# Hybrid encoder layer on one core: first norm on ScalarE, token tiles in pairs, early reload of the gated activations

## The chip, the cores and the metric

One core of a Trainium2 chip runs the whole layer in one launch. The metric is the device time of that launch in microseconds; runs of one kernel are told by their median. Engines: TensorE (PE; its weight loads PEld), VectorE (DVE), ScalarE (ACT), GpSimd (POOL), and SyncE (SP), whose queue issues all the DMAs.

## The reference, cut to what matters

```python
h   = layer_norm(DEEPNORM_ALPHA * x + mixed @ w_out, ln1_g, ln1_b)
up  = depthwise_conv(h @ w_up, conv_w, conv_b)          # 3 taps over tokens
a, val = split(up, 2)
out = layer_norm(DEEPNORM_ALPHA * h + (gelu(a, exact) * val) @ w_down, ln2_g, ln2_b)
```

All float32; 1024 tokens, model width 1024, hidden width 2816. `mixed` is the gated sum of a state-space branch and an attention branch. Everything ahead of `mixed @ w_out` (the first 750 us) is the same in both kernels.

## The kernel before

A tile framework places the instructions: it schedules the program with a timeline model of its own, so the order on every engine is its choice and moves when the code changes. Each float32 product is made of three reduced-precision products (hi·hi, hi·lo, lo·hi), so every operand is split: ScalarE copies it to the high part (`whi`, `ghi`, `t1h`), and VectorE or GpSimd subtracts that from the raw value (`wlo`, `glo`, `t1l`; `split`, L161).

**Out-projection** (`out_projection`). Eight token tiles of 128 go in three groups, (0,1,2), (3,4,5), (6,7), each with its own pass over the eight weight blocks `wo`; a tile needs two accumulators `pso` of 128x512. After a group, each tile is normed: `r` is loaded from x (L1046; three buffers), VectorE adds the accumulators (L156, two operations), takes the moments, and applies the norm with its gain and bias in four more operations (L156); the result is stored to DRAM as `hd` (L1051). PE transposes it (`ptr`, eight 128x128 per tile, four to an accumulator, L1055), and ScalarE copies four at a time into H (`hraw`, transposed hidden state, L159). For tiles 0 to 3 `b0h` and `b0l`, the split of tokens 0 to 511, are made from the accumulator too.

**Up-projection** (`up_projection`). 22 column blocks j, each with seven products of 12 matmuls (L1111) in a Strassen-like scheme: `first` and `second` use b11 and b21 (tokens 0 to 511, in `b0h`/`b0l`) directly, the other five use `t1`, `t2`, `t3`, `t4`, which are differences of quadrants of H (rows 0-511 or 512-1023 of the width, tokens 0-511 or 512-1023), and `b22`. For j = 0 and 1 `first` and `second`, 48 matmuls, come before the sums; then the differences are made over all tokens at once on VectorE and split on ScalarE, VectorE and GpSimd. Weight blocks come through a ring of three buffers (`raw`, `whi`, `wlo`). After each j, ScalarE and VectorE do the convolution on the accumulators (`cv`), and the gated result goes to DRAM as Gd[j].

**Down-projection** (`down_projection`). The same three groups of tiles; for each of 22 blocks k Gd[k] is read back (`graw`, L1229), split into `ghi` and `glo`, and multiplied with `wd` (L1277 to L1279). After a group each tile's `r2` (two buffers, loaded from `hd`, L1253) gets ALPHA and the accumulators, then the second norm and the store to the output.

Of the kernel before, what the change touches and what calls it, by code (L numbers as in the profile page):

```python
# [8 lines left out]
F32 = mybir.dt.float32  # L9
F32R = mybir.dt.float32r  # L10
# [52 lines left out]
def constants():  # L63
# [10 lines left out]
    small = np.zeros((P, 24), np.float32)  # L74
# [10 lines left out]
def prepare(inp):  # L85
# [46 lines left out]
    o["cbig"], o["csm"] = constants()  # L132
    return o


class K:
# [70 lines left out]
    def run(self, upto="all"):  # L207
        tc, nc, A = self.tc, self.nc, self.A
        with ExitStack() as ctx:
# [15 lines left out]
            self.csm = csm = cst.tile([P, 24], F32, name="csm")  # L225
# [684 lines left out]
    def layer_norm(self, r, g, b, wk, done, cols=(slice(0, 512), slice(512, 1024))):  # L910
# [9 lines left out]
        nc.vector.reciprocal(sd, sd)  # L920
        for h in range(2):
# [86 lines left out]
    def ffn(self, right):  # L1008
        with ExitStack() as ch:
# [6 lines left out]
            H = chr_.enter_context(self.pool("hraw", 1)).tile([P, KT, S], F32, name="hraw")  # L1016
            self.out_projection(b0, H)
            right.close()
            tp = ch.enter_context(self.pool("tp", 1, side="right"))
            self.up_projection(b0, H, tp, chr_)  # L1020
            chh.close()
        self.down_projection()

    def out_projection(self, b0, H):
        nc, A, tt = self.nc, self.A, self.tt
        mh, ml = self.mh, self.ml
        with ExitStack() as cx:
            wk = cx.enter_context(self.pool("owk", 3))
            lw = cx.enter_context(self.pool("lw", 1))
            pt = cx.enter_context(self.pool("ptr", 2, space=PSUM))  # L1030
            po = [cx.enter_context(self.pool(f"po{z}", 1, space=PSUM)) for z in range(6)]
            bank = {0: 0, 1: 2, 2: 4, 3: 0, 4: 2, 5: 4, 6: 0, 7: 2}
            gb = lw.tile([P, 2, D], F32, name="lngb")
            for z in range(2):
                nc.sync.dma_start(gb[:, z], A["ln"][z:z + 1].partition_broadcast(P))
            for tiles in ((0, 1, 2), (3, 4, 5), (6, 7)):
# [7 lines left out]
                for i in tiles:  # L1044
# [5 lines left out]
                    def transposed(q, c):  # L1050
                        nc.sync.dma_start(self.hd[i][:, c], r[:, c])  # L1051
                        tr = pt.tile([P, 4, P], F32, tag="t", name="ptr")
                        for j in range(4):
                            k = 4 * q + j
                            nc.tensor.transpose(tr[:, j], r[:, P * k:P * k + P], self.ident)  # L1055
                        rows = (slice(None), slice(4 * q, 4 * q + 4), slice(P * i, P * i + P))
# [7 lines left out]
    def up_projection(self, b0, H, tp, chr_):  # L1064

# [230 lines left out]
```

## Time and profile before

| what | value |
|---|---|
| median of 3 runs (lowest, highest) | 1544.2 us (1543.13, 1544.93) |
| the profiled execution, its own time | 1542.73 us |
| its span in the profile | 1540.6 us |
| granted TensorE clock, mean | 0.982 |
| PE busy | 1462.9 us, 95% of the span |
| VectorE, ScalarE, GpSimd busy | 982.4, 635.5, 634.8 us |
| chain that ended last, largest shares | PE 66%, VectorE 7%, DMA 3% |

A row of the timeline gives the start, the length, the engine, the line of the kernel, the operation with its result and operands, a count, and in brackets how long the engine stood idle before it and what it was waiting for. `x4` after a row means four such operations one behind the other, with their length together. Lines are those of the kernel before; in the changed kernel the same helpers stand two lines lower (L148, L158, L161, L165), the product is L1132, the transposes L1067.

### The profile page before, as it was taken

How to read it: one execution, taken by the hardware profiler on the slowest of the kernel's cores; microseconds unless marked ns; L12 is line 12 of the kernel's file. 1: busy time of each engine (PE TensorE's matmuls, PEld its weight loads, DVE VectorE, ACT ScalarE, POOL GpSimd, SP SyncE). 2: the span in 40 equal slices, each digit the busy share in tenths (PEclk: the TensorE clock that was granted, in tenths of full speed). 3: DMA queues.
4: the chain of work that ended last, by engine and by line, in shares of the span. 5: the costliest groups of instructions: out<-in, count | busy, mean ns of one | idle time of the engine just before them, and what ended most of it. 6: DMA issues, size and time to landing. Idle time of an engine off the chain costs nothing.

```text
span 1540.6 us, 19832 instructions
## 1 busy us (share of the span) xinstructions
PE 1462.9 (95%) x7210; PEld 1207.6 (78%) x7210; DVE 982.4 (64%) x1654; ACT 635.5 (41%) x1029; POOL 634.8 (41%) x363
## 2 busy tenths in 40 slices
PE   8989999989999998999997699999999998999998
PEld 6878778888877776788876478888888886888876
DVE  8967888460036367532588888888888884362363
ACT  5346675202154434543344444444444444433030
POOL 1397784353113101655544333344444334924020
PEclk9999999999999999999999799999999999999999
DMA  7643453765326123433565022222222227666141
GB/s 262 167 111 95 121 138 119 232 195 157 103 73 199 60 63 106 132 119 96 191 193 195 32 72 87 87 86 86 82 82 83 82 83 254 220 195 189 46 153 36
DMA packets 98691, 195.81 MB, mean 127 GB/s; under 512 B 11809, under 2 KB 45601, under 8 KB 98465
## 3 DMA queue, kind: packets, MB, share of 16 engines
q1 hardware_dynamic: 98592, 194.55, 40.1%
q8 instruction: 56, 0.92, 0.3%
q14 instruction: 43, 0.34, 0.1%
HBM read 145.87 MB, written 48.63 MB: 126 GB/s over the span
## 4 chain that ended last, share of the span: by engine, by line
PE 66%; DVE 7%; DMA 3%; issue 1%; ACT 1%; SPq 1%; POOL 1%; POOLq 0%; DVEq 0%; ACTq 0%
PE psup L1111 26%; PE psg L178 11%; PE pso L1277 6%; PE pso L1278 6%; PE pso L1279 6%; PE psv L178 6%; DVE r L156 2%; PE pso L178 2%; PE psS L178 1%; PE psab L178 1%; DVE hraw L146 1%; PE psp L181 1%; DMA og<-atd 1%; DMA raw<-wup 1%; DMA raw<-wd 0%
## 5 line engine op out<-in xcount | busy, mean ns | idle before, releaser
L163 POOL TENSOR_TENSOR wlo<-raw,whi 128x1024 fp32r<-128x1024 f32 x143 | 358.4, 2512 | 588.5 <-ACT whi L159 452.5
L159 ACT ACTIVATE whi<-raw 128x1024 fp32r<-128x1024 f32 (+1 forms) x174 | 174.5, 1004 | 259.4 <-PE psg L178 64.3
L178 PE MATMUL psg<-xh,whi 128*128 128x512 f32 x448 | 180.6, 403 | 4.5 <-DVE vout L146 4.3
L178 PE MATMUL psg<-xl,whi 128*128 128x512 f32 x448 | 180.0, 402 | 0.0
L178 PE MATMUL psg<-xh,wlo 128*128 128x512 f32 x448 | 179.5, 401 | 0.0
L1278 PE MATMUL pso<-wlo,ghi 128*128 128x512 f32 (+1 forms) x374 | 142.3, 381 | 2.5 <-POOL wlo L163 2.5
L1277 PE MATMUL pso<-whi,ghi 128*128 128x512 f32 (+1 forms) x374 | 136.8, 384 | 6.0 <-ACT ghi L159 5.6
L1279 PE MATMUL pso<-whi,glo 128*128 128x512 f32 (+1 forms) x374 | 140.2, 379 | 0.0
L163 DVE TENSOR_TENSOR glo<-graw,ghi 128x384 fp32r<-128x384 f32 (+1 forms) x66 | 58.9, 898 | 123.9 <-ACT ghi L159 110.4
L156 DVE SCALAR_TENSOR_TENSOR cv<-psup,cwt,cv 128x1023 f32<-128x1023 f32 x88 | 112.8, 1282 | 38.7 <-ACT cv L159 37.2
L178 PEld LDWEIGHTS psg<-xh,whi 128*128 128x128 f32 x448 | 85.6, 191 | 26.8 <-DVE vout L146 5.0
L178 PEld LDWEIGHTS psg<-xh,wlo 128*128 128x128 f32 x448 | 85.7, 191 | 20.6 <-issue 3.1
L824 DVE CUSTOM_DVE_ANT_0 sm<-psS,cbig 128x256 f32<-128x256 f32 (+2 forms) x96 | 31.6, 360 | 109.8 <-PE psS L178 105.2
L178 PEld LDWEIGHTS psg<-xl,whi 128*128 128x128 f32 x448 | 85.8, 192 | 20.1 <-issue 2.9
L1277 PEld LDWEIGHTS pso<-whi,ghi 128*128 128x128 f32 x374 | 70.8, 190 | 20.1 <-ACT ghi L159 6.0
L1278 PEld LDWEIGHTS pso<-wlo,ghi 128*128 128x128 f32 x374 | 71.1, 190 | 16.7 <-POOL wlo L163 2.9
L163 POOL TENSOR_TENSOR wlo<-wsum,whi 128x1024 fp32r<-128x1024 f32 x22 | 53.5, 2432 | 72.2 <-ACT whi L159 72.2
L1279 PEld LDWEIGHTS pso<-whi,glo 128*128 128x128 f32 x374 | 70.5, 189 | 14.0
L159 ACT ACTIVATE ghi<-graw 128x384 fp32r<-128x384 f32 (+1 forms) x66 | 31.8, 485 | 107.8 <-PE pso L1278 91.4
L1111 PE MATMUL psup<-b0h,wlo 128*128 128x512 f32 x176 | 68.7, 390 | 1.7 <-POOL wlo L163 1.7
L1111 PE MATMUL psup<-b0h,whi 128*128 128x512 f32 x176 | 68.8, 391 | 1.5 <-ACT whi L159 1.5
L159 ACT ACTIVATE sm<-sm,nm 128x256 f32<-128x256 f32 (+2 forms) x96 | 43.3, 451 | 63.6 <-DVE nm L151 51.4
(254 smaller groups left out, 3647.1 us busy)
## 6 DMA issues: line engine op xcount, KB each, us to landing
raw<-wup SPq DMA_DIRECT2D x46, 512.0 KB
raw<-wd SPq DMA_DIRECT2D x40, 512.0 KB
raw<-wo SPq DMA_DIRECT2D x24, 512.0 KB
Gd<-cv SPq DMA_DIRECT2D x22, 512.0 KB
graw<-Gd SPq DMA_DIRECT2D x44, 192.0 KB
raw<-wg SPq DMA_DIRECT2D x16, 512.0 KB
gd<-gout SPq DMA_DIRECT2D x32, 256.0 KB
qkd<-gout SPq DMA_DIRECT2D x48, 128.0 KB
```

Source lines behind the costliest of these rows:

```text
L146: (eng or self.nc.vector).tensor_tensor(out, a, b, op)
L156: self.nc.vector.scalar_tensor_tensor(out, a, s, b, op0, op1)
L159: self.nc.scalar.activation(out, a, f, **kw)
L163: lo_eng.tensor_tensor(lo, raw, hi.bitcast(F32), ALU.subtract)
L178: self.pin(self.nc.tensor.matmul(*args, **kw))
L181: self.pin(self.nc.tensor.transpose(out, a, self.ident))
L824: nc.vector.tensor_tensor_reduce(sm[:, e, 0:n], ps[e][:, 0:n], mask, 1.0, -3.0e38, ALU.add, ALU.max, accum_out=st[:, 256 + h:257 + h])
L1111: nc.tensor.matmul(ps, x[:, k], y[:, k], start=(k == 0 and n == 0 and not more), stop=(k == 3 and n == 2), skip_group_check=True)
L1277: mm(o, ah, w[0][:, c], start=(k == 0), stop=False, skip_group_check=True)
L1278: mm(o, ah, w[1][:, c], start=False, stop=False, skip_group_check=True)
L1279: mm(o, al, w[0][:, c], start=False, stop=(k == n - 1), skip_group_check=True)
```

## The change

1. The first norm: VectorE takes the moments, and ScalarE applies (r - mean)/sd in two 128x512 operations. `hd` now holds this value without gain and bias. Gain and bias are applied while the transposes are read out: eight ScalarE operations of 128x128 per tile, with a scale and a bias for each partition from a constant table, in place of two of 128x512. `b0h`, `b0l` are made from H.
2. The token groups are (0,4,1), (5,2,6), (3,7); after each tile from 4 on the four quadrant sums of its pair are made on VectorE (`token_sums`), so that the up-projection only splits. The load of the first norm's gain and bias is gone from here.
3. Gd[0] and Gd[1], tiles 0 to 2, are read back and split during the up-projection, into buffers of their own (`dg`).
4. The second residual: gain and bias of the first norm are loaded here (four broadcasts of 512 KB in place of two), GpSimd multiplies them by ALPHA, and for each tile multiplies and adds them to `r2`; VectorE then adds the accumulators. `p5`, `u2`, `v` of the up-projection lie in a pool that is opened after H is given up.

```diff
-            for tiles in ((0, 1, 2), (3, 4, 5), (6, 7)):
+            for tiles in ((0, 4, 1), (5, 2, 6), (3, 7)):
+                bank = {i: 2 * z for z, i in enumerate(tiles)}
...
+                    mv, sd = self.moments(r, wk, halves)
+                    nb = wk.tile([P, 1], F32, tag="nb", name="nb")
+                    self.stt(nb, mv[:, 0:1], -1.0, sd, ALU.mult, ALU.mult)
+                    for q, c in enumerate(halves):
+                        self.act(r[:, c], r[:, c], AF.Identity, scale=sd, bias=nb)
                         nc.sync.dma_start(self.hd[i][:, c], r[:, c])
                         tr = pt.tile([P, 4, P], F32, tag="t", name="ptr")
                         for j in range(4):
                             k = 4 * q + j
                             nc.tensor.transpose(tr[:, j], r[:, P * k:P * k + P], self.ident)
-                        self.act(H[rows], tr, AF.Copy)
+                            self.act(H[:, k, P * i:P * i + P], tr[:, j], AF.Identity,
+                                     scale=self.csm[:, 24 + k:25 + k], bias=self.csm[:, 32 + k:33 + k])
                         if i < 4:
-                            self.act(b0[0][rows], tr, AF.Copy)
-                            tt(b0[1][rows], tr, b0[0][rows].bitcast(F32), ALU.subtract)
-                    self.layer_norm(r, gb[:, 0], gb[:, 1], wk, transposed)
+                            self.act(b0[0][rows], H[rows], AF.Copy)
+                            tt(b0[1][rows], H[rows], b0[0][rows].bitcast(F32), ALU.subtract)
+                    if i >= 4:
+                        self.token_sums(H, T2, i - 4)
+    def token_sums(self, H, T2, i):
+        b11, b12, b21, b22 = (H[:, 4 * r:4 * r + 4, 512 * c + P * i:512 * c + P * i + P] for r in range(2) for c in range(2))
+        t2 = T2[:, :, P * i:P * i + P]
+        self.tt(b11, b12, b11, ALU.subtract)
+        self.tt(t2, b22, b11, ALU.subtract)
+        self.tt(b12, b22, b12, ALU.subtract)
+        self.tt(b21, b21, t2, ALU.subtract)
...
+            up = cu.enter_context(self.pool("uu", 1))
...
-                p5, u2, v = (self.pp.tile([P, 512], F32, tag=t, name=t) for t in ("p5", "u2", "v"))
+                p5, u2, v = (up.tile([P, 512], F32, tag=t, name=t) for t in ("p5", "u2", "v"))
+                if j == NFF - 2:
+                    self.early = [self.gated(dg, k, slice(0, 384)) for k in range(2)]
...
-            gb = lw.tile([P, 2, D], F32, name="lngb2")
+            gb = lw.tile([P, 4, D], F32, name="lngb2")
+            nc.gpsimd.tensor_scalar(gb[:, 0:2], gb[:, 0:2], ALPHA, None, ALU.mult)
...
                     nc.sync.dma_start(r, self.hd[i])
+                    for z, op in enumerate((ALU.mult, ALU.add)):
+                        tt(r, r, gb[:, z], op, nc.gpsimd)
                     for c in cut[i]:
-                        self.stt(r[:, c], r[:, c], ALPHA, ps[i, c.start], ALU.mult, ALU.add)
+                        tt(r[:, c], r[:, c], ps[i, c.start], ALU.add)
```

How the scheduler's order moved, at three places. First PE, where the out-projection (`pso`) ends and the up-projection (`psup`) begins, before:

```order
L1278 MATMUL pso<-wlo,mh 128x512
L1279 MATMUL pso<-whi,ml 128x512
L1277 MATMUL pso<-whi,mh 128x512
L1278 MATMUL pso<-wlo,mh 128x512
L1279 MATMUL pso<-whi,ml 128x512
L1111 MATMUL psup<-b0h,whi 128x512
L1111 MATMUL psup<-b0l,whi 128x512
L1111 MATMUL psup<-b0h,wlo 128x512
```

and with the change:

```order
L1300 MATMUL pso<-wlo,mh 128x512
L1301 MATMUL pso<-whi,ml 128x512
L1067 MATMUL ptr<-cbig,r 128x128 x26
L1132 MATMUL psup<-b0h,whi 128x512 x2
L1132 MATMUL psup<-b0l,whi 128x512
L1132 MATMUL psup<-b0h,wlo 128x512
L1132 MATMUL psup<-b0h,whi 128x512
```

Before, all the transposes ahead of this point were done and the first 36 `psup` followed at once, with the last two tiles' 16 transposes among the 48. Now 26 transposes stand there (tiles 2, 6, 3 and two of tile 7), and each but the first of an accumulator waits until ScalarE has read the one before it; the last six of tile 7 stand in twos after 20, 36 and 48 `psup`.

Second VectorE, from the last tile's transposes to the last split that the sums feed (`traw` is T2), before:

```order
L146 TENSOR_TENSOR hraw<-hraw 128x2x512
L163 TENSOR_TENSOR b22l<-hraw,b22h 128x1024
L146 TENSOR_TENSOR hraw<-hraw 128x2x512
L146 TENSOR_TENSOR wsum<-raw 128x512
L146 TENSOR_TENSOR hraw<-hraw,t_7970 128x512
L163 TENSOR_TENSOR t1l<-hraw,t1h 128x1024
L146 TENSOR_TENSOR hraw<-hraw,t_7976 128x512
L163 TENSOR_TENSOR t2l<-t_7970,t2h 128x512
L163 TENSOR_TENSOR t2l<-t_7976,t2h 128x512
L163 TENSOR_TENSOR t3l<-hraw,t3h 128x1024
L146 TENSOR_TENSOR wsum<-wsum,raw 128x512
L146 TENSOR_TENSOR raw<-raw 128x512
```

and with the change:

```order
L148 TENSOR_TENSOR hraw<-hraw 128x4x128
L148 TENSOR_TENSOR traw<-hraw 128x4x128
L148 TENSOR_TENSOR hraw<-hraw 128x4x128
L165 TENSOR_TENSOR b22l<-hraw,b22h 128x1024
L148 TENSOR_TENSOR hraw<-hraw,traw 128x4x128
L148 TENSOR_TENSOR wsum<-raw 128x512
L165 TENSOR_TENSOR t1l<-hraw,t1h 128x1024
L148 TENSOR_TENSOR wsum<-wsum,raw 128x512
L148 TENSOR_TENSOR raw<-raw 128x512
L165 TENSOR_TENSOR t2l<-traw,t2h 128x1024 x2
L165 TENSOR_TENSOR t3l<-hraw,t3h 128x1024
L165 TENSOR_TENSOR t4l<-hraw,t4h 128x1024
```

Before, the list had begun with four `hraw` and two `t` ahead of the first row, and went on with `t` and `t2l` of the last two blocks. Now four sums of 128x4x128 are all that is left of them, for the last pair alone.

Third GpSimd in the down-projection, where the first group of tiles ends (`r_11696` and `r_12244` are `r2` of tiles 2 and 3, `r_12294` of tile 4, `lngb` the gain and bias), now:

```order
L165 TENSOR_TENSOR wlo_11581<-raw,whi_11580 128x1024
L165 TENSOR_TENSOR wlo<-raw,whi 128x1024 x3
L148 TENSOR_TENSOR r_11696<-r_11696,lngb_10996 128x1024 x2
L148 TENSOR_TENSOR r_12244<-r_12244,lngb_10996 128x1024 x2
L165 TENSOR_TENSOR wlo<-raw,whi 128x1024 x2
L148 TENSOR_TENSOR r_12294<-r_12294,lngb_10996 128x1024
L165 TENSOR_TENSOR wlo<-raw,whi 128x1024
L148 TENSOR_TENSOR r_12294<-r_12294,lngb_10996 128x1024
L165 TENSOR_TENSOR wlo<-raw,whi 128x1024 x5
```

Before, only the weight splits `wlo<-raw,whi` stood here (15 in a row to the end of the program); now the products and sums of three tiles stand among them.

## Rows read from the trace of the kernel before

**Rows 1.** Windows: length; PE, PEld, DVE, ACT, POOL busy (instructions); clock, DMA share, GB/s.
```profile
845.00:865.00 20.00, 6.41 (x16) 4.41 (x17) 20.00 (x16) 8.37 (x10) 10.98 (x4) 0.57 0.13 46
...
909.00:1270.00 361.00, 361.00 (x1593) 299.01 (x1594) 317.62 (x285) 164.71 (x189) 142.51 (x57) 1.00 0.23 82
```

**Rows 2.** Timeline, PE, end of the out-projection: start, us, engine, line, operation.
```profile
827.16 0.39 PE L1279 MATMUL pso<-whi,ml 128*128 128x512 f32 x1
```

**Rows 3.** Timeline, PE, 860 to 862: in brackets the idle time before, and its releaser.
```profile
860.18 0.80 PE L1111 MATMUL psup<-t1l,whi 128*128 128x512 f32 x1 [6.70 <-DVE t1l L163]
860.77 0.63 PE L1111 MATMUL psup<-t1h,wlo 128*128 128x512 f32 x1
861.20 0.63 PE L1111 MATMUL psup<-t1h,whi 128*128 128x512 f32 x1
```

**Rows 4.** Lines with shapes apart, VectorE, 828 to 875: busy us, mean ns.
```profile
L146 DVE TENSOR_TENSOR hraw<-hraw 128x512 f32<-128x512 f32 x4 | 6.4, 1666 | 1.7 <-ACT hraw L159 1.7
...
L146 DVE TENSOR_TENSOR t<-hraw 128x512 f32<-128x512 f32 x4 | 2.6, 678 | 0.0
...
L163 DVE TENSOR_TENSOR t1l<-hraw,t1h 128x1024 fp32r<-128x1024 f32 x1 | 1.2, 1210 | 0.0
...
L915 DVE BATCH_NORM_STATS2 bst<-r 128x6 f32<-128x512 f32 x2 | 1.2, 657 | 0.0
```

**Rows 5.** Timeline, GpSimd, 850 to 875.
```profile
852.18 3.38 POOL L163 TENSOR_TENSOR t1l<-hraw,t1h 128x1024 fp32r<-128x1024 f32 x1 [2.32 <-ACT t1h L159]
...
871.76 2.38 POOL L163 TENSOR_TENSOR t4l<-hraw,t4h 128x1024 fp32r<-128x1024 f32 x1 [9.41 <-ACT t4h L159]
```

**Rows 6.** Lines with shapes apart, ScalarE, whole span.
```profile
L159 ACT ACTIVATE cv<-psup,cwt 128x1024 f32<-128x1024 f32 x44 | 52.7, 1198 | 3.5 <-DMA cwt<-cw 2.2 <-DVE psup L146 0.4
...
L159 ACT ACTIVATE whi<-wsum 128x1024 fp32r<-128x1024 f32 x22 | 23.3, 1061 | 90.4 <-PE psup L1111 90.0 <-DVE wsum L146 0.5
...
L159 ACT ACTIVATE XB<-X 128x128 f32<-128x128 f32 x16 | 4.9, 305 | 26.8 <-POOL X L616 26.7
...
L159 ACT ACTIVATE hraw<-ptr 128x512 f32<-128x512 f32 x16 | 9.2, 591 | 3.5 <-PE ptr L1055 3.5
...
L159 ACT ACTIVATE b0h<-ptr 128x512 fp32r<-128x512 f32 x8 | 4.8, 601 | 0.0
...
L159 ACT ACTIVATE sd<-mv,csm 128x1 f32<-128x1 f32 x16 | 4.7, 293 | 58.6 <-DVE mv L917 58.6
```

**Rows 7.** Lines with shapes apart, PE, 740 to 845.
```profile
L1055 PE MATMUL ptr<-cbig,r 128*128 128x128 f32 x64 | 9.1, 276 | 0.6 <-DVE b0l L146 0.4
```

**Rows 8.** Timeline, SyncE, VectorE and ScalarE: last x load, its reader, last eviction.
```profile
822.35 0.43 SPq L1046 DMA_DIRECT2D r<-x  x1
...
829.60 1.29 DVE L156 SCALAR_TENSOR_TENSOR r<-r,pso 128x512 f32<-128x512 f32 x2 [1.83 <-DMA raw<-wup]
...
843.97 1.07 ACT L159 ACTIVATE hraw<-ptr 128x512 f32<-128x512 f32 x2
```

**Rows 9.** Timeline, PE, VectorE and GpSimd, from the up- to the down-projection.
```profile
1278.31 0.39 PE L1111 MATMUL psup<-t4h,wlo 128*128 128x512 f32 x1
1284.31 0.80 PE L1277 MATMUL pso<-whi,ghi 128*128 128x512 f32 x1 [5.61 <-ACT ghi L159]
...
1279.82 3.96 DVE L156 SCALAR_TENSOR_TENSOR cv<-psup,cwt,cv 128x1023 f32<-128x1023 f32 x3
...
1271.54 2.40 POOL L163 TENSOR_TENSOR wlo<-raw,whi 128x1024 fp32r<-128x1024 f32 x1 [1.19 <-ACT whi L159]
```

**Rows 10.** Timeline, VectorE and SyncE, change of token groups in the down-projection.
```profile
1363.40 1.38 DVE L156 SCALAR_TENSOR_TENSOR r<-r,pso 128x512 f32<-128x512 f32 x2 [3.03 <-PE pso L1279]
...
1380.50 0.33 SPq L1253 DMA_DIRECT2D r<-hd  x1
```

**Rows 11.** Waits of PE, 1278 to 1540; timeline, VectorE, out-projection.
```profile
PE pso L1278 <- POOL wlo L163: 2.5, 2, 1.2
...
761.79 5.71 DVE L156 SCALAR_TENSOR_TENSOR r<-r,mv,lngb 128x512 f32<-128x512 f32 x2
```

More of the change, by code (lines that the diff above doesn't have):

```diff
@@ L73, in constants @@
     inv_freq = np.power(10000.0, -(p % 32) * 2.0 / HD)
-    small = np.zeros((P, 24), np.float32)
+    small = np.zeros((P, 40), np.float32)
     small[:, 0] = inv_freq
@@ L132, in prepare @@
     o["cbig"], o["csm"] = constants()
+    o["csm"][:, 24:40] = np.concatenate([g[n][0].reshape(KT, P).T for n in ("ln1_g", "ln1_b")], axis=1)
     return o
@@ L224, in run @@
             cbig = cst.tile([P, 320 + 3 * P], F32, name="cbig")
[L225 removed]
+            self.csm = csm = cst.tile([P, 40], F32, name="csm")
             self.band = cbig[:, 0:320]
@@ L907, in attention_out, with moments @@
         self.act(self.at[:, :, c], v, AF.Copy)
-    def layer_norm(self, r, g, b, wk, done, cols=(slice(0, 512), slice(512, 1024))):
+    def moments(self, r, wk, cols):
         nc = self.nc
@@ L920, in layer_norm @@
         nc.vector.reciprocal(sd, sd)
+        return mv, sd
+    def layer_norm(self, r, g, b, wk, done, cols=(slice(0, 512), slice(512, 1024))):
+        mv, sd = self.moments(r, wk, cols)
         for h in range(2):
@@ L1191, in up_projection, with gated @@
                 nc.sync.dma_start(self.Gd[j], cv[1])
+    def gated(self, pool, k, t, bufs=None, raws=None):
+        n = t.stop - t.start
+        g = pool.tile([P, 384], F32, tag="graw", name="graw", bufs=raws)
+        self.nc.sync.dma_start(g[:, 0:n], self.Gd[k][:, t])
+        a, b = (pool.tile([P, 384], F32R, tag=z, name=z, bufs=bufs) for z in ("ghi", "glo"))
+        self.split(g[:, 0:n], a[:, 0:n], b[:, 0:n], self.nc.vector)
+        return a, b
     def down_projection(self):
-        nc, A = self.nc, self.A
+        nc, A, tt = self.nc, self.A, self.tt
         with ExitStack() as cd:
@@ L1227, in operands @@
                             wts[z] = kept[z]
-                    g = wk.tile([P, 384], F32, tag="graw", name="graw", bufs=4)
-                    nc.sync.dma_start(g[:, 0:wd], self.Gd[k][:, t0:t0 + wd])
-                    a = wk.tile([P, 384], F32R, tag="ghi", name="ghi", bufs=KEEP + 1)
-                    b = wk.tile([P, 384], F32R, tag="glo", name="glo", bufs=KEEP + 1)
-                    self.split(g[:, 0:wd], a[:, 0:wd], b[:, 0:wd], nc.vector)
-                    w[k] = wts[k], a, b
+                    if t0 == 0 and k < 2:
+                        w[k] = (wts[k], *self.early[k])
+                    else:
+                        w[k] = (wts[k], *self.gated(wk, k, slice(t0, t0 + wd), KEEP + 1, 4))
                     return w[k]
```

54 lines of the change are left out of this document (19 added, 35 removed).

## The prediction

> **What bounds the kernel now.** I read first the shares of the chain that ended last: PE holds 66% of it, so the time is matmuls plus the places where PE stands still. Then the windows: from 909 to 1270 us PE starts 1593 operations in 361 us, 0.227 us each, without a gap [rows 1]. Nothing the change does there can gain. Third, PE's timeline around the two joints that the change touches. The out-projection ends at 827.16 + 0.39 = 827.5 [rows 2]; the last eviction of a transpose ends at 843.97 + 1.07 = 845.0 [rows 8]; the first matmul that needs `t1l` starts at 860.18 after 6.70 us of standing [rows 3]. In 845 to 865 PE is busy 6.4 of 20 us, at a granted clock of 0.57, and VectorE all 20 [rows 1]. So here the sums and splits on VectorE and GpSimd set the end; PE comes back at the lower of its two levels (1.2 instead of 2.4 GHz), matmuls 0.43 apart [rows 3]. The last split, `t4l` on GpSimd, ends at 871.76 + 2.38 = 874.1 [rows 5]. The second joint: the last `psup` starts at 1278.31, the first `pso` of the down-projection at 1284.31, 5.61 us of it idle for `ghi` [rows 9]. Third place, the change of token groups in the down-projection: nothing waits there now; all waits for `wlo` from 1278 to the end are 2.5 us [rows 11].
>
> **Part 1, out- to up-projection.** All times count from the last `pso`, now at 827.5. 38 transposes instead of 48 stand ahead of the last `pso`: ten at 0.14 us (9.1 us over 64 [rows 7]) = 1.4 us gained. Against it, transposes now go one by one with ScalarE. An eviction of 128x128 with two pointer operands has no row: the plain one takes 0.305, and two pointers add 1.198 - 1.061 = 0.14 at 128x1024 [rows 6], so 0.44 (bounds 0.305, the plain one, and 0.59, the 128x512 one [rows 6]). Two accumulators alternate, so a pair costs about 0.28 for the transpose [rows 7], 0.44, and 0.1 for the two hand-overs: 0.8 us. The Trainium skill, ScalarE: Activation LUTs, section What ACT_TABLE_LOAD costs, gives each pointer operand some 93 ns on top of 186 ns and 0.83 ns per element, which would make 0.48 us here; the pairs on the chain below would then add half a microsecond. Runs of three and five transposes in the third group have few matmuls between them; I take 2 us of standing there. Net +0.5: the last `pso` ends at 828.
>
> From there the chain is:
> - ScalarE has a weight copy in front (1.06 [rows 6]); then tile 2's eight transposes, four pairs, 3.2 us: 3.5 with some overlap.
> - Only now is tile 7's `r` buffer free, so its x load is issued at 3.5. Before, this load was issued at 822.35 and its reader started at 829.60, 7.25 us later, after waiting for it [rows 8]. I take 6.5, since fewer loads stand around it: 10.
> - Two additions of the accumulators 1.3 [rows 8], moments 1.3 [rows 4] and an estimated 0.2, root 0.3 [rows 6], two small operations 0.3, two norm operations on ScalarE 1.1 (pairs of 0.59 [rows 6], overlapped): 14.5.
> - On ScalarE tile 3's evictions stand behind that norm: four pairs 3.2, `b0h` 0.6 [rows 6], `b0l` on VectorE 0.7 [rows 4]: 19. Here the first `psup` starts; before it started at once. Tile 3 is in the last group, and `first` needs tokens 0 to 511 complete, so the 48 independent matmuls no longer cover the norm of the last tiles.
> - 48 `psup` at 0.227 = 10.9, at the lower level in their first part (+2.5, from 0.43 against 0.227 over about a dozen, as after 860.18), three pairs of transposes 1, last evictions 0.9: 34.5, that is 862.5. Before: 845.0. **The last tile is 17.5 us later.**
>
> Behind it the chain is shorter. VectorE's list, now: three sums, `b22l`, one sum, `wsum`, `t1l`, two more of `wsum`, `t2l` twice, `t3l`, `t4l`: seven of 128x512 at 0.68 and six of 128x1024 at 1.21 [rows 4] = 12.0 us. Before: 19 and 6, 20.2 us. Both lose time to GpSimd: an operation of VectorE on two SBUF tensors that meets a GpSimd subtract waits for its end. Four `hraw` took 1.67 each instead of 0.68 [rows 4], 4 us, and GpSimd's own `t1l` 3.38 instead of 2.40 [rows 5, 9]. Before, the way from the last eviction to `t4l` was 29.1 us, 8.9 more than the work. I take 8 more again, as the same four GpSimd splits remain: 12 + 8 = 20, so `t4l` ends at 882.5 instead of 874.1: **+8.4**. PE has t1 and t2 of j = 0 to do until then (24 matmuls); the next product, b22, waits for `p5`, whose buffer now lies in memory that H gives up only after `t4l`, where PE could go on before. What PE so has left to do after `t4l` it mostly does while weights are on their way; I add 0.6. Sum of part 1: **+9 us**. Bounds: the load at 4 us and VectorE losing only half as much give +2; evictions of 0.59 and a loss of 12 us give +14.
>
> **Part 2, up- to down-projection.** `ghi` and `glo` of k = 0 and 1 are there early; the first weight split stands at 1271.54 [rows 9] and does not change. PE then has k = 0 and 1 of two tiles, 24 matmuls, 5.4 us, until tile 2's accumulators are free, when VectorE has read `cv` (1279.82 + 3.96 = 1283.8 [rows 9]). So the 5.61 us of standing go, and about 2 of the low clock behind them: **-7.5**. Bounds: -8.5, everything, and -3 if a weight or an accumulator comes late.
>
> **Part 3, GpSimd in the down-projection.** 16 operations of 128x1024 at 2.40 [rows 9] and one twice as long: 43 us more on an engine that is not the bound there. Their cover is the lead of the weight splits. Five stand early in group one, where blocks are several ahead; the rest at the two changes of groups, where the lead is used up (rival two). I take **+1.5**, bounds 0 and +6. The VectorE additions are as long as before. The four broadcasts are 1 MB more, beside transfers that are not waited for: nothing.
>
> Everything else is the same work: nothing from 909 to 1270.
>
> **Sum.** 9 - 7.5 + 1.5 = +3 on the profiled execution, 1542.73, gives 1545.7; the median shown is 1.5 higher, so **1547.2 us**. A measurement tells about 0.2% (3.1 us) from no change, so this case alone (1542 to 1552) is as often no change as slower.
>
> **Rivals.**
> 1. *The sums win (faster).* If VectorE and GpSimd no longer meet, 6 us of the 8 above go, and a load of 4 us in place of 6.5 takes 2.5 more: part 1 falls to about +0.5, the sum to -6: 1538. For it: the longest losses fell on the 128x512 sums, most of which are now made earlier. Against it: the four GpSimd splits still stand beside VectorE's.
> 2. *GpSimd blocks the weights (slower).* At a change of groups tile 3's `r2` can be loaded only when tile 1's output is stored. Tile 0's addition starts at 1363.40, that load is issued at 1380.50, 17.1 us later [rows 10]; with 3 us to land (estimate) 20. Behind it in GpSimd's queue stand its two operations, 4.8, and the split of k = 3, 2.4: 27.3. PE needs that split 120 matmuls after tile 0's last, 27.2 us. It decides to the microsecond: each one that the load or the norm is later, PE stands, at both changes of groups. The norm may be later, since its operations with two SBUF tensors meet GpSimd's: such a pair took 5.71 us beside two weight splits [rows 11], against 1.4. 4 us at each change is +7 more: 1554. The Trainium skill, GPSIMD Engine Reference, section Specifications, says that GpSimd shares its SBUF interfaces with VectorE and meets its two-input operations; by that rule this rival is likelier, and the 5.71 agrees.
> 3. *The early reload gives little (slower).* A weight or an accumulator still holds the first `pso`: part 2 is -3, the result 1551.5.
>
> **Chances.** My case 0.45, rival one 0.30, rival two 0.17, rival three 0.08. Faster by over 0.2%: nearly all of rival one, 0.28. Within: half of my case and a little of the others, 0.29. Slower: the other half, rivals two and three, 0.43. The range takes rival one at its centre and rival two with one microsecond more: 1537.5 to 1555.5.
>
> **What would show it.** Right: the first `psup` some 19 us after the last `pso`; the last `hraw` eviction near 862; `t1l` near 874, `t4l` near 882; no idle over 1 us between `psup` and the down-projection's `pso`; no wait for `wlo` above 2 us after 1300. Wrong: a first `psup` within 10 us, `t4l` before 876 (rival one), or PE standing for `wlo` near 1390 and 1478, 27 and 26 us after the first tile of a group is done (rival two).

## The result and the profile after

The changed kernel takes 1587.7 us (median of 4 runs, 1587.2 to 1594.5), the kernel before beside it 1544.6 (4 runs): a ratio of 1.0281, 95% interval 1.0262 to 1.0300. It is **slower by 43 us**. The prediction had the sign as the likeliest of three, but its range ended at 1555.5.

The profiled execution has a span of 1585.4 us against 1540.6, 44.8 more. Four points in PE's timeline divide that sum, and every later comparison uses them:

| stretch | before | after | difference | predicted |
|---|---|---|---|---|
| start to last `pso` of the out-projection | 827.16 | 831.55 | +4.4 | +0.5 |
| from there to the first `psup` that needs `t1l` | 33.0 | 50.75 | +17.7 | with the row above +9 |
| from there to the last `psup` | 418.1 | 427.5 | +9.3 | 0 |
| last `psup` to the end | 262.3 | 275.6 | +13.3 | -7.5 and +1.5 |

The first row is within what this stretch varies: in e1, e7 and e11 below, whose edits all lie behind it, the last `pso` starts at 829.0, 834.8 and 834.5, and in the three kernels that differ from the one before by unused bytes alone at 826.9, 829.8 and 834.9. The last two rows need one correction: with the change twelve `pso` of the down-projection, 2.7 us of work, stand ahead of the last `psup`, and none did before. So 2.7 us of the third row belong to the fourth.

**The first joint**, PE's timeline of the changed kernel, for [rows 2, 3] (start, us, engine, line, operation, idle time before and its releaser):

```profile
831.55 0.39 PE L1301 MATMUL pso<-whi,ml 128*128 128x512 f32 x1
...
851.92 0.83 PE L1067 MATMUL ptr<-cbig,r 128*128 128x128 f32 x2 [0.20 <-ACT hraw L161]
852.79 0.80 PE L1132 MATMUL psup<-b0h,whi 128*128 128x512 f32 x1
...
882.30 0.79 PE L1132 MATMUL psup<-t1l,whi 128*128 128x512 f32 x1 [6.56 <-DVE t1l L165]
```

After the last `pso` come 26 transposes, and PE waits for ScalarE's `hraw` at nearly every second one. The last row of two (0.83, with 0.20 of waiting ahead; the one before it starts at 850.90) shows the pace: 1.02 us from one pair to the next. The first `psup` starts 21.2 us after the last `pso` (predicted 19), and `t1l` is waited for until 882.30, where it was 860.18 before.

SyncE, VectorE and ScalarE in the same stretch, for [rows 8]:

```profile
835.43 0.33 SPq L1052 DMA_DIRECT2D r<-x  x1
...
843.20 1.28 DVE L158 SCALAR_TENSOR_TENSOR r<-r,pso 128x512 f32<-128x512 f32 x2
...
867.94 0.79 ACT L161 ACTIVATE hraw<-ptr,csm 128x128 f32<-128x128 f32 x2
```

The last x load is issued at 835.43 instead of 822.35, its reader starts 7.8 us later, and the last eviction ends at 867.94 + 0.79 = 868.7 instead of 845.0.

VectorE's list from there to `t1l`, and GpSimd's splits, for [rows 4, 5]:

```profile
868.42 2.59 DVE L148 TENSOR_TENSOR hraw<-hraw 128x512 f32<-128x512 f32 x1 [2.33 <-ACT hraw L161]
871.11 2.69 DVE L148 TENSOR_TENSOR traw<-hraw 128x512 f32<-128x512 f32 x1
873.73 2.87 DVE L148 TENSOR_TENSOR hraw<-hraw 128x512 f32<-128x512 f32 x1
...
878.86 3.39 DVE L165 TENSOR_TENSOR t1l<-hraw,t1h 128x1024 fp32r<-128x1024 f32 x1
```

```profile
873.22 2.82 POOL L165 TENSOR_TENSOR t1l<-hraw,t1h 128x1024 fp32r<-128x1024 f32 x1
881.11 3.41 POOL L165 TENSOR_TENSOR t4l<-hraw,t4h 128x1024 fp32r<-128x1024 f32 x1
```

VectorE has little left, as foreseen, but the three sums, which run beside GpSimd, take 2.6 to 2.9 us instead of 0.68, and `t1l` itself 3.39 instead of 1.21 [rows 4]. (Between them stand `b22l`, one more sum and a `wsum`.) `t4l` on GpSimd ends at 884.5, where 882.5 was predicted.

**The up-projection** from 960 to 1270, the view by windows of the changed kernel, for [rows 1]:

```profile
960.00:1270.00 310.00, 309.33 (x1333) 250.02 (x1332) 265.36 (x238) 136.24 (x158) 120.61 (x48) 1.00 0.23 82
```

PE is busy 309.33 of the 310 us and the granted clock is 1.00, as before. But it starts 1333 operations in 309.33 us, 0.2321 us each; before it was 361 / 1593 = 0.2266 [rows 1]. That is 0.0054 more on each of 1848 matmuls, 10 us, and nothing in the prediction spoke of it.

**The second joint** has lost its standing, as predicted; PE's timeline, for [rows 9]:

```profile
1301.62 1.09 PE L1299 MATMUL pso<-whi,ghi 128*128 128x512 f32 x4
...
1309.76 0.40 PE L1132 MATMUL psup<-t4h,wlo 128*128 128x512 f32 x1
1309.99 1.09 PE L1299 MATMUL pso<-whi,ghi 128*128 128x512 f32 x4
```

The next `pso` follows the last `psup` by 0.23 us, where 5.61 us of standing were. Twelve `pso` already stand among the `psup` ahead of it, the first four at 1301.62 and eight more from 1305.34.

**The down-projection**, PE's longest waits at the two changes of groups, for [rows 11]:

```profile
1416.08 1.66 PE L1299 MATMUL pso<-whi,ghi 128*128 128x512 f32 x6 [1.78 <-ACT whi L161]
1421.53 0.74 PE L1300 MATMUL pso<-wlo,ghi 128*128 128x512 f32 x1 [3.79 <-POOL wlo L165]
1436.45 0.80 PE L1300 MATMUL pso<-wlo,ghi 128*128 128x512 f32 x1 [4.85 <-POOL wlo L165]
...
1524.02 0.80 PE L1300 MATMUL pso<-wlo,ghi 128*128 128x512 f32 x1 [6.81 <-POOL wlo L165]
```

Together with 1.89 us at 1347.85 and 0.74 at 1385.11 these are 19.9 us of waiting for weight splits. What GpSimd does at that time, and SyncE's issues:

```profile
1406.48 5.09 POOL L148 TENSOR_TENSOR r<-r,lngb 128x1024 f32<-128x1024 f32 x2 [9.38 <-DMA r<-hd]
1413.54 5.19 POOL L148 TENSOR_TENSOR r<-r,lngb 128x1024 f32<-128x1024 f32 x2 [1.96 <-DVE bst L917]
1418.66 5.59 POOL L165 TENSOR_TENSOR wlo<-raw,whi 128x1024 fp32r<-128x1024 f32 x2
1431.75 2.35 POOL L148 TENSOR_TENSOR r<-r,lngb 128x1024 f32<-128x1024 f32 x1 [7.49 <-DMA r<-hd]
```

```profile
1422.10 3.07 SPq L1280 DMA_DIRECT2D out_dram<-r  x2
1428.09 0.32 SPq L1273 DMA_DIRECT2D r<-hd  x1
```

GpSimd stands 9.38 and 7.49 us in front of a product whose `r` has not been loaded; the load at 1428.09 was issued only after the output store of 1422.10 had freed its buffer. Behind the products stand the weight splits. And the norm that must free that buffer is slow, as VectorE's rows beside GpSimd show (without it, at 1401.33 in the same trace, such a pair takes 1.42 us):

```profile
1414.37 4.91 DVE L158 SCALAR_TENSOR_TENSOR r<-r,mv,lngb 128x512 f32<-128x512 f32 x2
1419.39 5.41 DVE L158 SCALAR_TENSOR_TENSOR r<-r,sd,lngb 128x512 f32<-128x512 f32 x2
```

### The profile page after: what moved, and what is told of

It is laid out like the page before. It is cut to its first block, busy times and chain, and to the rows that moved or that the text cites. A ratio compares the mean times of both kernels' runs of the same rounds, so it can differ in the third digit from the quotient of the medians.

```text
span 1585.4 us, 19905 instructions
## 1 busy us (share of the span) xinstructions
PE 1487.6 (94%) x7210; PEld 1212.0 (76%) x7210; DVE 975.1 (62%) x1630; ACT 659.3 (42%) x1091; POOL 687.3 (43%) x380
## 4 chain that ended last, share of the span: by engine, by line
PE 60%; DVE 16%; DMA 8%; ACT 6%; issue 4%; POOL 3%; SPq 2%; DVEq 0%; ACTq 0%; POOLq 0%
PE psup L1132 24%; PE psg L180 11%; PE psv L180 6%; PE pso L1300 4%; PE pso L1301 4%; PE pso L1299 4%; DMA raw<-wd 2%; PE pso L180 2%; PE psS L180 1%; DVE w L148 1%; POOL wlo L165 1%; PE psab L180 1%; DVE pss L148 1%; DVE c L148 1%; POOL r L148 1%
## 5 line engine op out<-in xcount | busy, mean ns | idle before, releaser
L165 POOL TENSOR_TENSOR wlo<-raw,whi 128x1024 fp32r<-128x1024 f32 x143 | 362.8, 2541 | 509.9 <-ACT whi L161 374.7
L1300 PE MATMUL pso<-wlo,ghi 128*128 128x512 f32 (+1 forms) x374 | 145.8, 390 | 18.3 <-POOL wlo L165 18.1
L1301 PE MATMUL pso<-whi,glo 128*128 128x512 f32 (+1 forms) x374 | 144.2, 387 | 0.0
L165 DVE TENSOR_TENSOR glo<-graw,ghi 128x384 fp32r<-128x384 f32 (+1 forms) x66 | 67.3, 1026 | 124.7 <-ACT ghi L161 124.7
L1299 PE MATMUL pso<-whi,ghi 128*128 128x512 f32 (+1 forms) x374 | 124.6, 380 | 1.8 <-ACT whi L161 1.8
L180 PEld LDWEIGHTS psg<-xl,whi 128*128 128x128 f32 x448 | 85.0, 190 | 19.9 <-issue 3.0
L148 POOL TENSOR_TENSOR r<-r,lngb 128x1024 f32<-128x1024 f32 x16 | 42.6, 2665 | 78.2 <-DMA r<-hd 68.0
```

The costliest lines, as they stand in the source:

```text
L148: (eng or self.nc.vector).tensor_tensor(out, a, b, op)
L165: lo_eng.tensor_tensor(lo, raw, hi.bitcast(F32), ALU.subtract)
L180: self.pin(self.nc.tensor.matmul(*args, **kw))
L1299: mm(o, ah, w[0][:, c], start=(k == 0), stop=False, skip_group_check=True)
L1300: mm(o, ah, w[1][:, c], start=False, stop=False, skip_group_check=True)
L1301: mm(o, al, w[0][:, c], start=False, stop=(k == n - 1), skip_group_check=True)
```

## The experiments

Every time is a median; differences to the changed kernel are taken from its 1587.7, and each run had the kernel before beside it (1543.5 to 1546.6). "Stretch" means the stretches of the table above.

**e1, the r2 products on VectorE.**

```diff
-                        tt(r, r, gb[:, z], op, nc.gpsimd)
+                        tt(r, r, gb[:, z], op)
```

> The changed kernel (1587.7 us) with one edit: the two products r2*g and r2+b in front of each token tile's norm in the down-projection run on VectorE instead of GpSimd. Theory (GpSimd's queue stands still while an r2 load is outstanding, and the weight splits behind it come late): PE's waits for wlo from 1340 us to the end fall from 18.4 us to under 2, the low clock behind them goes too, and the time falls by 20 to 26 us, to 1562-1568. Rival (the splits are late because weights arrive late, or because both engines meet in memory): the waits stay above 10 us and the time falls by under 8 us, to 1580 or more.

1570.9 us, ratio to before 1.0187 (1.0171 to 1.0203): 17 us less than the change, where 20 to 26 were expected. From the last `psup` to the end it takes 264.1 us instead of 275.6. PE's waits after 1290 (in total, times, longest):

```profile
PE pso L1300 <- POOL wlo L165: 3.8, 3, 1.9
PE pso L1299 <- DVE cv L158: 2.5, 1, 2.5
PE pso L1301 <- DVE glo L165: 1.7, 1, 1.7
PE pso L1300 <- DVE wlo L165: 1.6, 1, 1.6
```

The 18 us of waiting for `wlo` are down to 3.8. By the medians the products on GpSimd cost 17 us. The profiles differ by 16.0, and 11.5 of that lies behind the last `psup`; the rest lies in stretches that the edit does not touch. Beside the 3.8, the other rows hold 5.8 us of smaller waits.

**e2, the kernel before with 64 unused bytes.**

```diff
-            self.csm = csm = cst.tile([P, 24], F32, name="csm")
+            self.csm = csm = cst.tile([P, 40], F32, name="csm")
```

> The kernel before (1544.6 us) with one edit: the constants tile csm is 40 instead of 24 columns wide, nothing reads the new ones. It moves every later tile on the left side of SBUF (weights and b0 among them) by 64 bytes, and none on the right side (t1 to t4, b22). Theory A (the step of the psup matmuls grew from 0.2267 to 0.2321 us in the changed kernel because the left tiles moved by 64 bytes against the right ones): step 0.231 to 0.233, time +8 to +11 us, 1552-1556. Theory B (it grew because the pool of the early G tiles moved t1 to t4 and b22): step 0.2267, 1543-1546. Theory C (neither, something that runs beside): as B.

1556.6 us, ratio 1.0095 (1.0064 to 1.0125): 13 us slower, from a tile that is 64 bytes wider. The window of the up-projection:

```profile
960.00:1270.00 310.00, 310.00 (x1338) 250.50 (x1337) 267.51 (x240) 137.63 (x160) 119.02 (x48) 1.00 0.23 82
```

310 / 1338 = 0.2317, as in the changed kernel. That is what theory A said, and not what theories B and C said.

**e3, the changed kernel with 128 bytes.** `csm` is 56 columns wide instead of 40.

> The changed kernel (1587.7 us) with one edit: csm is 56 columns wide instead of 40, so that the left tiles lie 128 bytes and not 64 from where they lay before. Theory A (64 bytes between left and right tiles): the psup step falls from 0.2321 back to about 0.227 us, time -9 to -11 us, 1577-1579. Theory B (the early G pool moved the right tiles) and theory C (something that runs beside): step 0.232, 1586-1589.

1585.2 us, ratio 1.0278 (1.0258 to 1.0298), and a step of 0.2314: a miss for theory A as it was put. It is not the 64 bytes as such.

**e4, the early reload alone** in the kernel before: the pool `dg`, `gated`, and its call at the last column tiles but one, word for word those of the change.

> The kernel before (1544.6 us) with the early G reload alone: the pool of six small tiles on the right side of SBUF, filled for k = 0 and 1 while the last column tiles of the up-projection run. No wider constants, no new groups, no work moved to GpSimd. The 5.6 us of standing at the start of the down-projection go and the low clock behind them: -7 to -9 us if the psup step stays 0.2267 (theories A and C), so 1536-1538. If the pool's place slows psup (theory B), its step is 0.232 and +10 stands against that: 1545-1548.

1539.05 us over 10 runs, ratio 0.9975 (0.9959 to 0.9992); step 0.2267, so theory B falls again. From the last `psup` to the end 254.6 us instead of 262.3, which is -7.7 (the last `psup` starts at 1283.36, the span is 1538.0). The whole gains only 4.5 by the medians. The last `psup` comes 5.1 us later in the profiled execution: 2.0 of it lies ahead of the last `pso`, and 2.7 are the twelve `pso` that now stand among the last `psup`, the first four here:

```profile
1275.43 1.07 PE L1288 MATMUL pso<-whi,ghi 128*128 128x512 f32 x4
```

So of the 7.7 us 2.7 are work that moved to the other side of the mark, and 5.0 are gained. From the last `pso` to the end it is 4.6 us (708.8 against 713.4), as by the medians.

**e5, the scale and shift columns elsewhere.**

```diff
-            self.csm = csm = cst.tile([P, 40], F32, name="csm")
+            self.csm = csm = cst.tile([P, 24], F32, name="csm")
...
+            lw = cx.enter_context(self.pool("lw", 1))
+            gs = lw.tile([P, 16], F32, name="gs")
+            nc.sync.dma_start(gs, A["csm"][:, 24:40])
...
-                                     scale=self.csm[:, 24 + k:25 + k], bias=self.csm[:, 32 + k:33 + k])
+                                     scale=gs[:, k:k + 1], bias=gs[:, 8 + k:9 + k])
```

> The changed kernel (1587.7 us) with csm 24 columns wide again; the 16 scale and shift columns lie in a small tile of the out-projection's own, so that the weights and b0 lie at the same place within 2048 bytes as before the change (b0 6144 bytes lower). Theory A (the place of the left tiles, down to 64 bytes, sets the psup step): step 0.2267, time -9 to -13 us, 1575-1579. Rival (a shift of 128 bytes took only 0.0007 off the step, so the cause in the changed kernel is the early G pool and the place of t1 to t4 and b22, and the 64 bytes matter only beside the old place): step 0.231 to 0.232, 1585-1588.

1577.7 us, ratio 1.0200 (1.0179 to 1.0220): -10 us. The window from 960 to 1270:

```profile
960.00:1270.00 310.00, 310.00 (x1369) 256.69 (x1368) 273.71 (x245) 141.99 (x164) 122.98 (x49) 1.00 0.24 85
```

310 / 1369 = 0.2264. The last `pso` to the last `psup` takes 467.9 instead of 478.2 us.

**e6, transposes ahead of their evictions.**

```diff
                         for j in range(4):
                             k = 4 * q + j
                             nc.tensor.transpose(tr[:, j], r[:, P * k:P * k + P], self.ident)
+                        for j in range(4):
+                            k = 4 * q + j
                             self.act(H[:, k, P * i:P * i + P], tr[:, j], AF.Identity,
```

> The changed kernel with the four transposes of a half tile issued ahead of its four evictions, not in turns with them; the same instructions otherwise. Theory (the turns cost 0.9 to 1.3 us a pair on the chain from the last pso to the last eviction, where ScalarE's 0.47 alone would do, and PE stands between): the last hraw eviction comes 5 to 9 us sooner than 868.4, t1l too, PE's waits on ScalarE's hraw before 830 vanish, and the time falls by 5 to 10 us, to 1578-1583. Rival (the chain is held by the x loads and the norms of the last two tiles, and psup work fills PE's gaps in any case): last eviction within 2 us of 868, time within 3 us of 1587.7.

1568.1 us, ratio 1.0149 (1.0119 to 1.0178): -20 us, twice the upper end of what was expected. From the last `pso` to the last `psup` it takes 461.1 us; before it was 451.2, and the longer step and the twelve `pso`, both still in this kernel, are more than the difference. So **the joint costs nothing any more**. (The profiled execution is the slowest of the four, 1575.3 us; what it has over the median lies behind the last `psup`, 283.6 us against 275.6 in the change, where the edit does nothing.) ScalarE's last evictions, and on PE the first tile's transposes and the first matmul that needs `t1l`:

```profile
842.33 2.88 ACT L161 ACTIVATE hraw<-ptr,csm 128x128 f32<-128x128 f32 x8
847.49 1.56 ACT L161 ACTIVATE hraw<-ptr,csm 128x128 f32<-128x128 f32 x4
```

```profile
776.85 1.03 PE L1067 MATMUL ptr<-cbig,r 128*128 128x128 f32 x8
...
867.56 0.39 PE L1134 MATMUL psup<-t1l,whi 128*128 128x512 f32 x1
```

Eight evictions in a row take 2.9 us, where four pairs in turns take four times 1.02 us. That is 1.2 us a tile and not 20. The larger part shows in the first tile's eight transposes, in e6 one row of 1.03 us at 776.85, in the changed kernel these:

```profile
771.44 0.27 PE L1067 MATMUL ptr<-cbig,r 128*128 128x128 f32 x1
772.01 0.27 PE L1067 MATMUL ptr<-cbig,r 128*128 128x128 f32 x1
777.86 0.38 PE L1067 MATMUL ptr<-cbig,r 128*128 128x128 f32 x2
782.90 0.27 PE L1067 MATMUL ptr<-cbig,r 128*128 128x128 f32 x1
...
788.28 0.27 PE L1067 MATMUL ptr<-cbig,r 128*128 128x128 f32 x1
```

All eight go over 16.8 us: in PE's list, which is fixed beforehand, some 20 `pso` now stand between one pair and the next. PE hardly waits there, but the tile keeps its r buffer all the while, and the x loads that follow are late. In e6 the last two are issued at

```profile
815.69 0.33 SPq L1052 DMA_DIRECT2D r<-x  x1
822.51 0.37 SPq L1052 DMA_DIRECT2D r<-x  x1
```

and in the changed kernel at 827.94 and 835.43, 12 to 13 us later. In e6 the last eviction ends at 849.1, 21 us after the last `pso`, where the change needs 37, and PE comes to `t1l` at 867.56 with no wait for it (its longest there is 4.5, for `t2l`). The edit changes the whole list, so the 20 us are those of the new order, not of single hand-overs.

**e7, three buffers for r2.** One line: `bufs=3` in the tile `r2`.

> The changed kernel with three buffers for r2 in place of two in the down-projection; GpSimd still does the two products of each tile. Theory one (GpSimd's queue stands for the load of r2, whose buffer waits for an output store): its idle time for r2 loads between 1390 and 1450 falls from 16.9 us to under 8, PE's waits for wlo from 18 to under 9, time -8 to -14 us, 1574-1580. Rival (GpSimd's 43 us of products by themselves, and the slow VectorE norms beside them, make the splits late): waits stay above 13 us, time -4 us or less.

1600.6 us, ratio 1.0350 (1.0329 to 1.0372): 13 us **slower**, which neither theory had. SyncE's queue at the start of the down-projection, and PE:

```profile
1320.03 0.33 SPq L1202 DMA_DIRECT2D Gd<-cv  x1
1322.95 1.75 SPq L1221 DMA_DIRECT2D lngb<-ln  x4
1324.75 2.55 SPq L1208 DMA_DIRECT2D graw<-Gd  x4
```

```profile
1333.71 0.80 PE L1299 MATMUL pso<-whi,ghi 128*128 128x512 f32 x1 [16.99 <-ACT ghi L161]
```

The buffer moved the tile of the broadcasts, and in SyncE's queue the G loads now stand behind these, which are issued only after the last store of the up-projection (1320.03). In the change the first of these loads went out at 1293.61. So PE stands 17 us for a `ghi`. GpSimd's standing for r2 loads did not fall either (11.93 and 5.24 us in front of its products at 1424.84 and 1435.31, against 9.38 and 7.49). The run does not tell the two theories apart; e11 does.

**e8, four mends with the old token groups.** e1, e5 and e6 together, and `(0, 1, 2), (3, 4, 5), (6, 7)`.

> The changed kernel with four edits together: r2 products on VectorE (measured alone: -17 us), scale and shift columns in a tile of the out-projection's own (as e5), transposes ahead of evictions (as e6), and the old token groups 0 1 2 / 3 4 5 / 6 7, so that b0 is complete while tiles 6 and 7 are still normed and the first psup no longer waits for the last norm. If the four costs found so far add up: 1587.7 - 17 - 10 - 7 - 6 = 1548, between 1540 and 1556. If the early G reload is all that is left of the change, the result is that of the kernel before with it alone, 1539. If the norm on ScalarE and the eviction in eight pieces cost by themselves, it stays above 1556.

1544.0 us over 10 runs, ratio 0.9981 (0.9967 to 0.9995), inside the range of the sum. Two of the sum's terms, 7 and 6, were not yet measured; with the 20 of e6 in their place it is 1587.7 - 17 - 10 - 20 = 1541. The costs add up.

**e9 and e10, what in the place counts.** The kernel before, in e9 with `csm` 32 columns wide, in e10 with 40 and an empty tile on the other side:

```diff
+            right.enter_context(self.pool("pad", 1, side="right")).tile([P, 112], F32, name="pad")
             tp = ch.enter_context(self.pool("tp", 1, side="right"))
```

> The kernel before with csm 32 columns wide: the left tiles move by 32 bytes (the weights then start at multiples of 1024), the right ones not at all. The step of the psup matmuls tells two theories apart. Relative theory (what counts is where weights and moving tile lie to each other within 512 bytes; before they lie alike): step 0.230 to 0.233. Absolute theory (what counts is how the weights' own rows lie against multiples of 64 or more): step 0.2267 or less. The single time is read only roughly: 1552-1556 or 1543-1546.

> The kernel before with csm 40 columns wide, as in the run that was 13 us slower, and an empty tile of 448 bytes at the right edge of SBUF, which moves t1 to t4 and b22 down by 448 bytes, so that they again lie at the same place within 512 bytes as the weights. Relative theory: step 0.2267, time about 1544. Absolute theory: step 0.232, 1553-1556.

e9 took 1552.1 us with a step of 0.2318, e10 1549.8 with 0.2267 (one run each; the last `pso` of e10 comes 7.8 us later than before, and its way from there to the last `psup` is 452.0 us, before 451.2, e9 459.3). The window of e10:

```profile
960.00:1270.00 310.00, 310.00 (x1369) 256.68 (x1368) 272.49 (x246) 142.97 (x163) 123.15 (x49) 1.00 0.23 82
```

In every kernel the step is short where the two places agree and long where they do not, as the relative theory says; the absolute one expected the opposite of both e9 and e10. The addresses are those of the programs' memory layout, the step is the mean between neighbouring `psup` starts (some 1250 pairs each):

| kernel | weights `whi`, modulo 512 | `t1` to `t4`, `b22`, modulo 512 | step, us |
|---|---|---|---|
| before, e4, e5, e8, e12, e13 | 480 | 480 | 0.2267 |
| e10 | 32 | 32 | 0.2267 |
| e9 | 0 | 480 | 0.2318 |
| e2, after | 32 | 480 | 0.2321 |
| e3 | 96 | 480 | 0.2314 |

One thing seems to speak against it: `b0h` and `b0l` move along with the weights, so by the theory their products should stay at 0.2267, and in e2 and the changed kernel their mean is 0.2289. But only the first five steps of a run of such matmuls are long (0.2283 to 0.2348 in e2 and the change); from the sixth on they are 0.2264 to 0.2269. So what is left of the slower step there comes right behind the other products.

**e11, three tiles of eight on GpSimd.**

```diff
-                        tt(r, r, gb[:, z], op, nc.gpsimd)
+                        tt(r, r, gb[:, z], op, nc.gpsimd if i < 3 else None)
```

> The changed kernel (1587.7 us) with the r2 products of tiles 0, 1, 2 on GpSimd as in the change and those of tiles 3 to 7 on VectorE. Queue theory (what costs is GpSimd standing for r2 loads at the two changes of groups; the products whose loads come early cost next to nothing): as with all of them on VectorE, 1569-1573, waits for wlo after 1340 under 6 us. Load theory (each product costs, by GpSimd's time and by VectorE's slower operations beside it): the three of eight tiles keep some 6 us of the 17, 1575-1579.

1570.3 us, ratio 1.0168 (1.0148 to 1.0187): as much gained as with all products on VectorE. From the last `psup` to the end it takes 259.5 us. PE's waits for GpSimd's `wlo` after 1290:

```profile
PE pso L1300 <- POOL wlo L165: 4.4, 5, 1.9
```

The first three tiles' products cost nothing that shows, and the load theory falls as it was put. The queue theory has the time right, but not quite the reason: only the loads of tiles 0 and 1 come early (1303.63 and 1304.58). That of tile 2 is issued at 1404.17, GpSimd stands 8.70 us for it, and still PE waits at most 1.9 us for a split. One stand at a change of groups is within the lead of the splits; what costs is the products of tile 3 and later, which come behind it and behind each other. Whether they cost by standing or by their own 5 us a tile is not separated by a run; in the trace of the change both stand ahead of the late splits.

**e12, scale and shift of the residual in the out-projection**, on GpSimd, before the tile is stored.

```diff
+                    for z, op in enumerate((ALU.mult, ALU.add)):
+                        tt(r, r, gb[:, z], op, nc.gpsimd)
+                    nc.sync.dma_start(self.hd[i], r)
```

> A version that keeps what paid and moves what cost: norm on ScalarE, transposes ahead of evictions, token groups 0 4 1 / 5 2 6 / 3 7, sums made there, early G, scale and shift columns in a tile of the out-projection's own; the products r*g and r+b for the residual run on GpSimd in the out-projection, before the tile is stored, and the down-projection is that of before. If GpSimd's 38 us of products lie beside other work there: the early reload's -7.7 and a joint as in the run with transposes first (about 0), 1534-1539 against 1544.6. If they hold the r buffers, and with them the last x load, or slow VectorE's sums: each 5 us of that shows, 1540-1550.

1564.25 us over 6 runs, ratio 1.0130 (1.0105 to 1.0155): the bad case, and more. The down-projection, without the products and their two broadcasts, takes 254.0 us from the last `psup` to the end, as in e4; all of the loss lies before it. GpSimd holds the r buffers: the last x load is issued at 842.51 (e6: 822.51), and VectorE's subtractions beside it slow down, one of several:

```profile
837.04 2.82 DVE L148 TENSOR_TENSOR hraw<-hraw 128x512 f32<-128x512 f32 x1
```

**e13, the change with three mends**: e5, e6 and e11, its own token groups kept.

> The changed kernel with its own token groups and three edits: scale and shift columns in a tile of the out-projection's own (alone -10), the four transposes of a half ahead of its evictions (alone -20), and the r2 products of tiles 3 to 7 on VectorE (alone -17). If these three are the whole account, they add up: 1587.7 - 47 = 1541, between 1536 and 1545, level with the kernel before or a little faster, as the early reload alone is. If the change's groups or the norm on ScalarE cost something that the three do not cover, and that the run with the old groups hid: above 1547.

1540.1 us over 12 runs beside 1546.6, ratio 0.9963 (0.9946 to 0.9980): **48 us faster than the change, and a little faster (0.4%) than the kernel before**. PE's timeline:

```profile
821.46 0.39 PE L1306 MATMUL pso<-whi,ml 128*128 128x512 f32 x1
...
860.58 0.39 PE L1137 MATMUL psup<-t1l,whi 128*128 128x512 f32 x1
...
1272.02 0.39 PE L1137 MATMUL psup<-t4h,wlo 128*128 128x512 f32 x1
```

From the last `pso` to the last `psup` 450.6 us, to the end 263.0. With tile 3 last, the first `psup` (839.39) still comes 17.9 us after the last `pso`, and that costs nothing here. It and the early reload alone (e4, 0.9975) can't be told apart; both beat the kernel before by a few us.

## Why the prediction was wrong

The stretches of the profiles differ by +22.1 (to `t1l`), +9.3 (from there to the last `psup`) and +13.3 (to the end), 44.7 of 44.8. With the twelve `pso` put back behind the last `psup` (2.7 us) these are +22.1, +6.6 and +16.0. The +6.6 is the longer step, 9.8 by e5 (417.7 us for this stretch against 427.5), less some 3 us behind `t1l`, where PE stands 4.0 us against 5.5 before; the rest of these 3 us was not traced. The +16.0 is the early reload, -5.0 by e4, and +21.0 for the other changes of the down-projection (275.6 less 254.6 in e4).

- **"Nothing the change does there can gain", and "nothing from 909 to 1270".** The first is right, the second is a step that failed and had no row: +10. The change of `csm` from 24 to 40 columns stood in the full diff and was costed at nothing without a word; e2, e5, e9 and e10 show that the place of the tiles in SBUF sets the step.
- **Part 1, +9.** The chain's dates were good: the last eviction 34.5 us after the last `pso`, measured 37.2; `t4l` at 882.5, measured 884.5. The step that failed is where the difference was taken. The text dates `t1l` "near 874", 13.8 later than in [rows 3], and still charges +8.4, the delay of `t4l`. But PE waits for `t1l`, and `t4l` was not waited for before (it ended at 874.1, and its product began at 881.68) nor after (884.5 and 902.27). By its own dates the term was +13.8; the rest is a last `pso` 3.9 later than assumed, which this stretch varies by, 2.7 more from there to the last eviction (1.3 of it a reader that came 7.8 instead of 6.5 after its load), and some 2 from there to `t1l`, where VectorE ran beside GpSimd.
- **The pairs.** Foreseen at 0.8 us, measured 0.88 to 1.02 where they follow each other. The eviction alone was sized well: the row's estimate was 0.44, and the 64 evictions of the change from 740 to 880 us have a mean of 0.450. The prediction's estimate by the Trainium skill, ScalarE: Activation LUTs, section What ACT_TABLE_LOAD costs, was 0.48; this trace lies a little below it. What the text did not see is what makes the chain late. It took the late load from the order (3.5 us after the last `pso`, measured 3.9) and counted a tile's turns as "four pairs, 3.2 us". But ahead of the last `pso` a tile's four pairs stand 5 us apart in PE's list, each behind some 20 matmuls, and the r buffers, the x loads and the norms of the last two tiles wait for them. Taking the turns away (e6) was worth 20 us, nearly all of what this joint cost.
- **"Tile 3 is in the last group", 19 us without `psup`.** True as a date and harmless as a cost: e13 has the same 18 us and loses nothing.
- **Part 2, -7.5.** Right in its mechanism, as the standing went, but some 2.5 us too large. The -7.7 of e4 that seems to confirm it holds the twelve `pso`; the gain is 5.0, as new waits of 2.6 us for `glo` come behind it.
- **Part 3, +1.5.** This step failed most, by 19.5: the lead of the weight splits was taken to cover GpSimd's products. **Rival two** names the mechanism, at +7. It gave the place nearly: PE begins to stand for a split of GpSimd at 1417.74, 29 us after the first tile of a group is done (1388.64), with "27" foreseen. But it counted one block at each change. GpSimd's products for each later tile wait in turn, each behind another load, so that the waits at the first change go on to 1436, and at the second one alone is 6.81 us long (1524.02). GpSimd's standing for r2 loads was 68 us in all. Of these, 51 stand in one piece ahead of the product at 1505.12, and PE waited for no split meanwhile; the other 17 are the 9.38 and 7.49 shown above:

```profile
L148 POOL TENSOR_TENSOR r<-r,lngb 128x1024 f32<-128x1024 f32 x16 | 42.6, 2665 | 78.2 <-DMA r<-hd 68.0 <-DVE r L158 8.0 <-DVE bst L917 2.0
```

- **Norms beside GpSimd.** Rival two took 5.71 for a pair; measured 4.91 and 5.41, which lengthens the way to the store that frees the buffer. The Trainium skill, GPSIMD Engine Reference, section Specifications, says that the two engines share their SBUF interfaces and that VectorE operations with two SBUF inputs meet GpSimd there; the case agrees with these two pairs.

Not settled: why the down-projection of e1, e11 and e13 (264.1, 259.5 and 263.0 us) is still 5 to 10 us longer than that of e4 (254.6). PE stands 10.8, 7.7 and 11.4 us there, against 5.2 in e4. As e12 has 254.0, the rest belongs to the products, or to the two broadcasts more that they need, and not to the other parts of the change; which of the two it is was not tried. Nor is it known which part of the chip makes the step depend on the places.

## What to carry to other kernels

Take the delay of a chain at the value that its consumer waits for, not at the chain's end. When you compare a stretch of two traces, count first whether the same work lies in it. In a diff, every tile that changes its size is a term: look at where the later tiles come to lie, and compare the step of the busiest loop before and after. Work that is given to an idle engine brings its waits into that engine's queue, so look first for what stands behind it there; and hand small PE and ScalarE operations over in blocks rather than in turns, since each turn can cost a place in the busy engine's list.

## What the runs showed of the hardware

- The step of a 128x512 fp32r matmul is 0.2267 us when weights and moving tile start at the same place in SBUF modulo 512 bytes, and 0.2314 to 0.2321 when they are 32, 64 or 128 bytes apart (modulo 512). The clock is granted in full both times. In the changed kernel the `b0` products, whose tile moved along with the weights, have 0.2289 (0.2264 to 0.2269 from the sixth of a run on) and the others 0.2333. Shown for `psup` alone; other distances were not tried.
- 128x128 evictions on ScalarE that follow each other go at 0.36 us (eight in 2.9), though each one is recorded with 0.45 to 0.47.
- In a stretch that no edit touches, the same instructions end up to 6 us earlier or later from one profiled execution to another (last `pso` at 829.0 to 834.8 in the change, e1, e7 and e11); a difference of a few us needs the same points in both traces and more than one run.
